# A folded Fourier mixer: modulation sums spread anew, pairs of tiles folded in two operations, the two pairs leaving in the other order

## The chip, the cores and the metric

The kernel runs on one core of one Trainium2 chip. The metric is the device time of one execution in microseconds (us). Three runs of the kernel before gave 2249.22, 2250.83 and 2252.3 us; the median is 2250.83 us. The profile is of one execution of its own.

## The reference

One inference step of a two-layer backbone over 128 context tokens and 512 latent tokens of 1024 channels, in float32. Every layer is a half-step SwiGLU feed-forward part (hidden width 2816), a token mixer, and another half-step feed-forward part. Each of these six sub-layers is wrapped in the same frame:

```
h = rmsnorm(x, g_pre) * (1 + scale) + shift
x = x + gate * rmsnorm(sublayer(h), g_post)
```

Shift, scale and gate come from `silu(cond) @ w_mod + b_mod`, nine vectors of 1024 per layer, one set for the context tokens and one for the latent tokens. The mixer of layer 0 is a Fourier mixer: `u = h @ w_in`, then the real part of a two-dimensional discrete Fourier transform over the positions of a sequence and the 128 channels of each of eight groups, then `@ w_out`; context and latent tokens are separate sequences. The mixer of layer 1 is attention. The outputs are the tokens and the keys and values of the context tokens.

## The kernel before

The six sub-layers are numbered n = 0 to 5; n = 1 is the Fourier mixer and n = 4 the attention. The 640 tokens are five tiles of 128: tiles 0, 1, 3 and 4 hold latent tokens, tile 2 the context. Every float32 product is three matmuls on pieces: `split` (L258) rounds a value on ScalarE (hi, L260) and takes the rest on VectorE (lo, L261), and `mm3` (L271) multiplies hi by hi, hi by lo and lo by hi (L274 to L276).

**Weights.** All weights of the program stand in one list of units of 512 KB. `unit(i)` (L204) hands out unit i and first sends those up to three further on: `send` (L211) starts a load into one of four raw buffers (`raw_tile`, L199, on the SP queue, in order), combines columns where the unit asks for it (L226 to L228, L236, L238, L243) and splits the result into one of six weight buffers, or, where its kind has "block" in it, into two tiles of a general ring of twenty. The ring holds hidden values and tokens as well.

**Modulation sums.** One vector of 128 outputs of `w_mod` is one "sum" here: a load of 512 KB into a raw buffer, and for each of the two conditions one VectorE operation over 1024 elements (`gemv`, L471 to L476). 128 of them wait in a list (`background`, L1589 to L1595), and `behind(n)` (L253) issues the next n. Before, this happens only in the feed-forward parts: after each tile of the first four slices of the second product, `BEHIND[n]` in all per part (L44, L956).

**A feed-forward part** (`ffn`, L728) goes through 22 hidden chunks; after every fourth chunk its part of the second product runs for all five tiles (`w2`, L905), and after the last six chunks for tiles (0, 1), (2), (3) and (4). The end of a tile hands its two PSUM banks to `boundary`, which starts a chain.

**A chain** (`chain`, L608) is the frame above for one tile: squares and their sum (L620), gate (L621, L624), root on GpSimd (L597), the new x (L627), squares of it (L641), the multiplication by the inverse root (L644), eight transposes on TensorE (L665), then scale and shift (L686 on ScalarE, L688 on VectorE), and the split into the next sub-layer's h. The result stands in `wide_y`, 1024 columns per tile. `TURNS` (L45) says after how many ns of matmul work the transposes are put into TensorE's order. From n = 0 to n = 1 the tokens of tiles 0 and 1, and of 3 and 4, are also folded into their difference and sum (L650, L651) before the transposes, and the second tile of a pair gets the scale without the shift (L680, L682). Tile 0 keeps its x in four pieces, so each operation on it is four.

**The Fourier mixer** (`fourier`, L1068): `pair_in(0)` multiplies pair (0, 1) by the folded `four_in` (L236 and L238 fold its columns; two operations of L238, one for each half of the groups), then the context, then `pair_in(1)`. `positions(m)` and `channels(m)` do the transform for four m, each a position step ahead of the channel step. Then the product with eight units of `four_out`: `own` (the even rows of the context, L1234), `pair_out(0)`, the odd rows of the context (`ctx`, L1240), `pair_out(1)`; each is followed by the chains of its tiles. The next feed-forward part takes tiles 0, 1 and half of tile 2 first (`finish(0)`, L942, then 320 columns), the others later.

The order on each engine is not the order of the text alone: a scheduler places what is ready by priority, `high_priority` (all of a chain) ahead of the rest, and `behind_of` or `issue_after` ties an instruction behind another. Each engine then goes through its order and waits at each instruction for what it needs.

## Time and profile before

| what | us |
|---|---|
| median of three runs | 2250.83 |
| the profiled execution's own time | 2249.42 |
| span of the profiled execution | 2247.6 |
| TensorE (PE) busy | 2173.4 |
| VectorE (DVE) busy | 1753.9 |
| ScalarE (ACT) busy | 1175.2 |

The rows below come from views of this one execution. A row of the windows view names a stretch (us from the start of the span) and its length, then the busy time and number of instructions of PE, PE's weight loads, DVE, ACT and GpSimd (POOL), the granted clock of TensorE as a share of full speed, the share of the DMA engines, and GB/s. A row of the groups view names line, engine, operation, the tiles written and read, the shape and count, then busy us, mean ns of one, and idle us before them. A row of the timeline has start and duration in us and, in brackets, the idle time before it and what ended it. A row of the waits view names who waited for whom, us in all, times and the longest.

### The profile page before, as it was taken

How to read it: one execution, taken by the hardware profiler on the slowest of the kernel's cores; microseconds unless marked ns; L12 is line 12 of the kernel's file. 1: busy time of each engine (PE TensorE's matmuls, PEld its weight loads, DVE VectorE, ACT ScalarE, POOL GpSimd, SP SyncE). 2: the span in 40 equal slices, each digit the busy share in tenths (PEclk: the TensorE clock that was granted, in tenths of full speed). 3: DMA queues.
4: the chain of work that ended last, by engine and by line, in shares of the span. 5: the costliest groups of instructions: out<-in, count | busy, mean ns of one | idle time of the engine just before them, and what ended most of it. 6: DMA issues, size and time to landing. Idle time of an engine off the chain costs nothing.

```text
span 2247.6 us, 34637 instructions
## 1 busy us (share of the span) xinstructions
PE 2173.4 (97%) x13299; PEld 1999.0 (89%) x13299; DVE 1753.9 (78%) x3255; ACT 1175.2 (52%) x2222; POOL 44.4 (2%) x95
## 2 busy tenths in 40 slices
PE   7999899898989999999999999999999999999998
PEld 5989889886689999998999999989999899999997
DVE  5988988978788898896988998776555686766684
ACT  4534444454654554545545545466788654455452
POOL 0000000000000000000000000000000000000000
PEclk9999999998989999999999999999999999999999
DMA  8244344434324344444334344523333323322232
GB/s 311 86 158 169 123 151 159 150 107 133 115 81 155 127 158 143 136 160 150 117 132 147 130 149 156 192 82 96 116 110 113 102 92 103 113 91 88 94 127 99
DMA packets 85862, 293.25 MB, mean 130 GB/s; under 512 B 9696, under 2 KB 14656, under 8 KB 85568
## 3 DMA queue, kind: packets, MB, share of 16 engines
q1 hardware_dynamic: 85152, 290.39, 38.6%
q8 instruction: 104, 1.70, 0.3%
q10 hardware_dynamic: 544, 0.66, 0.1%
q14 instruction: 62, 0.51, 0.1%
HBM read 275.49 MB, written 11.58 MB: 128 GB/s over the span
## 4 chain that ended last, share of the span: by engine, by line
PE 82%; DVE 9%; DMA 4%; ACT 3%; issue 2%; POOL 0%; SPq 0%; DVEq 0%; POOLq 0%; ACTq 0%
PE main L274 11%; PE main L275 11%; PE main L276 11%; PE score L274 7%; PE score L276 7%; PE score L275 7%; PE turn L274 4%; PE turn L275 4%; PE turn L276 4%; PE sum L276 4%; PE sum L275 4%; PE sum L274 4%; DVE junk L473 3%; DMA raw<-in_w_mod_t 2%; DVE lo L261 2%
## 5 line engine op out<-in xcount | busy, mean ns | idle before, releaser
L260 ACT ACTIVATE hi<-raw 128x1024 fp32r<-128x1024 f32 (+1 forms) x388 | 370.8, 968 | 291.5 <-PE score L275 88.6
L261 DVE TENSOR_TENSOR lo<-raw,hi 128x1024 fp32r<-128x1024 f32 (+1 forms) x388 | 429.2, 1113 | 105.2 <-ACT hi L260 103.6
L275 PE MATMUL main<-lo,ring 128*128 128x512 f32 (+5 forms) x1089 | 408.8, 376 | 8.1 <-DVE lo L261 8.1
L274 PE MATMUL main<-hi,ring 128*128 128x512 f32 (+4 forms) x1089 | 411.1, 379 | 2.0 <-DVE ring L627 1.2
L276 PE MATMUL main<-hi,ring 128*128 128x512 f32 (+5 forms) x1089 | 407.8, 375 | 0.0
L473 DVE SCALAR_TENSOR_TENSOR junk<-raw,wide 128x1024 bf16<-128x1024 f32 x256 | 313.1, 1223 | 77.5 <-DMA raw<-in_w_mod_t 73.5
L274 PE MATMUL score<-ring,hi 128*128 128x320 f32 x916 | 287.3, 314 | 16.6 <-ACT hi L260 12.2
L276 PE MATMUL score<-ring,lo 128*128 128x320 f32 x916 | 287.0, 313 | 6.0 <-DVE lo L261 5.8
L275 PE MATMUL score<-ring,hi 128*128 128x320 f32 x916 | 286.0, 312 | 0.0
L275 PEld LDWEIGHTS main<-lo,ring 128*128 128x128 f32 (+2 forms) x1089 | 204.7, 188 | 47.2 <-DVE lo L261 9.2
L274 PEld LDWEIGHTS main<-hi,ring 128*128 128x128 f32 (+2 forms) x1089 | 203.7, 188 | 43.6 <-DVE ring L627 1.4
L276 PEld LDWEIGHTS main<-hi,ring 128*128 128x128 f32 (+2 forms) x1089 | 204.6, 188 | 40.0 <-issue 0.6
L274 PE MATMUL turn<-ring,hi 128*128 128x320 f32 x672 | 208.6, 310 | 0.1
L275 PE MATMUL turn<-ring,hi 128*128 128x320 f32 x672 | 208.4, 310 | 0.0
L274 PE MATMUL sum<-ring,hi 128*128 128x320 f32 x672 | 207.5, 309 | 0.3 <-DVE left L868 0.3
L275 PE MATMUL sum<-ring,hi 128*128 128x320 f32 x672 | 207.7, 309 | 0.0
L276 PE MATMUL sum<-ring,lo 128*128 128x320 f32 x672 | 207.7, 309 | 0.0
L276 PE MATMUL turn<-ring,lo 128*128 128x320 f32 x672 | 207.5, 309 | 0.0
L929 ACT ACTIVATE y<-main 128x512 f32<-128x512 f32 x160 | 94.2, 591 | 208.9 <-PE main L276 207.7
L274 PEld LDWEIGHTS score<-ring,hi 128*128 128x128 f32 x916 | 175.0, 191 | 19.9 <-ACT hi L260 13.4
L276 PEld LDWEIGHTS score<-ring,lo 128*128 128x128 f32 x916 | 174.6, 191 | 8.1 <-DVE lo L261 8.1
L275 PEld LDWEIGHTS score<-ring,hi 128*128 128x128 f32 x916 | 175.2, 191 | 0.7
(312 smaller groups left out, 4123.6 us busy)
## 6 DMA issues: line engine op xcount, KB each, us to landing
raw<-in_w SPq DMA_DIRECT2D x272, 512.0 KB, 3.8
raw<-in_w_mod_t SPq DMA_DIRECT2D x128, 512.0 KB, 3.5
raw<-in_qkv SPq DMA_DIRECT2D x26, 512.0 KB, 3.5
spill<-ring SPq DMA_DIRECT2D x12, 640.0 KB, 3.0
ring<-spill SPq DMA_DIRECT2D x12, 640.0 KB, 7.3
raw<-in_bias SPq DMA_DIRECT2D x16, 448.0 KB, 3.8
first<-in_w_mod_k SPq DMA_DIRECT2D x8, 512.0 KB, 8.3
ring<-in_w_mod_k SPq DMA_DIRECT2D x8, 512.0 KB, 10.2
```

What stands on the lines that cost most here:

```text
L260: a = self.nc.scalar.activation(hi, src, AF.Copy)
L261: self.last_split = a, self.nc.vector.tensor_tensor(lo, src, hi.bitcast(F32), op=ALU.subtract)
L274: mm(out, whi, xhi, start=start, stop=False)
L275: mm(out, whi, xlo, start=False, stop=False)
L276: self.latest = mm(out, wlo, xhi, start=False, stop=stop)
L473: last = self.nc.vector.scalar_tensor_tensor(out=self.junk, in0=raw, scalar=1.0, in1=self.wide[:, cond, :], op0=ALU.mult, op1=ALU.mult, ac ...
L929: nc.scalar.activation(place(i, a), ps[a], AF.Copy)
```

## The change

- `BEHIND` of the first feed-forward part goes from 48 to 36. The twelve sums are issued elsewhere: four in the last slice of the same part's second product, three in `pair_in(1)`, five in the loop over `channels`.
- The fold of a pair of tiles takes two operations that multiply by the inverse root at the same time, one for the difference and one for the sum, in place of a multiplication and two operations. The difference has the other sign; the sine matrix `diffs` is negated for it. The first tile of a pair, tile 2, and in the Fourier mixer's chains tile 3, are multiplied by the inverse root on ScalarE.
- After the transposes of a pair the first tile's eight scale-and-shift operations are all on ScalarE; the second tile's eight become two on VectorE, one for each PSUM bank, with the scale read with a stride of zero. The splits of a pair cover both tiles in one.
- The inner columns of `four_in` are stored with the two halves of the groups interleaved, so that the second fold operation is one; the even columns are cut at 256 and 520 rather than at 260 and 520. The cosine and sine matrices of the channel step are stored to match.
- `pair_out(1)` comes first, then `own`, `ctx` and `pair_out(0)`. Tiles 3 and 4 take the columns 0 to 255 of the next h and tiles 0 and 1 the last 256 (`SWAPPED`, `slot`); the next feed-forward part begins with tiles 3, 4 and 2.
- Of `four_out`, units 3 and 4 lie in the ring in place of 6 and 7, and the loop over `channels` calls for units 0 to 3 (and with them up to unit 6).
- `TURNS` has a row of its own for n = 0 and n = 1; the transposes of pair (3, 4) in n = 0 and of tiles 2, 3 and 4 in n = 1 come later.

The core of the diff:

```diff
 SLICES = ((0, 4), (4, 8), (8, 12), (12, 16), (16, 22))
 EARLY = 2
-BEHIND = (48, 0, 36, 36, 0, 8)
+BEHIND = (36, 0, 36, 36, 0, 8)
 TURNS = (
+    {1: 15500, 2: 9200, 4: 15500},
+    {0: 10500, 1: 14000, 2: 10500, 3: 12500, 4: 15500},
     {0: 10500, 1: 14000, 2: 9200, 3: 11000, 4: 13000},
-    {1: 15500, 2: 9200, 4: 12500},
...
 CTX_TILE = 2
+SWAPPED = (3, 4, 2, 0, 1)
...
             raw = self.raw_tile(src)
             a, b = raw[:, one], raw[:, two]
             if "rows" not in kind:
-                a = raw[:, :528].rearrange("p (a x) -> p a x", a=2)[:, :, :256].rearrange("p a (g c) -> p a g c", c=64)
-                a, b = a[:, :, :, 1:], raw[:, 520:].rearrange("p (a g c) -> p a g c", a=2, c=63)
+                a, b = a.rearrange("p (m c) -> p m c", m=4)[:, :, 2:], raw[:, 520:].rearrange("p (m c) -> p m c", m=4)
             nc.vector.tensor_tensor(b, a, b, op=ALU.subtract)
-            for x, y in [(a, b)] if "rows" in kind else [(a[:, i], b[:, i]) for i in range(2)]:
-                nc.vector.scalar_tensor_tensor(out=x, in0=x, scalar=2.0, in1=y, op0=ALU.mult, op1=ALU.subtract)
+            nc.vector.scalar_tensor_tensor(out=a, in0=a, scalar=2.0, in1=b, op0=ALU.mult, op1=ALU.subtract)
...
-    def finish(self, half):
-        for i in ((0, 1, 2), (3, 4))[half]:
-            self.close(i)
+    def finish(self, half, first=(0, 1, 2)):
+        for i in range(TILES):
+            if (i in first) == (not half):
+                self.close(i)
...
+    def slot(self, n, i):
+
+        return SWAPPED[i] if n == 2 else i
...
-        place = self.wide_y[:, i * D : (i + 1) * D]
+        slot = self.slot(n + 1, i)
+        place = self.wide_y[:, slot * D : (slot + 1) * D]
...
-            for t, lo, hi in x:
-                nc.vector.tensor_scalar_mul(place[:, lo:hi], t, r)
             pair = next((p for p in PAIRS if i in p), None) if n == 0 else None
-            if pair and i == pair[0]:
-                return
-            if pair:
-                a, b = (self.wide_y[:, j * D : (j + 1) * D] for j in pair)
-                tt(b, a, b, op=ALU.subtract)
-                nc.vector.scalar_tensor_tensor(out=a, in0=a, scalar=2.0, in1=b, op0=ALU.mult, op1=ALU.subtract)
-                if i == pair[1] == 1:
+            if pair and i == pair[1]:
+                first, t = self.wide_y[:, pair[0] * D : i * D], x[0][0]
+                nc.vector.scalar_tensor_tensor(out=place, in0=t, scalar=r, in1=first, op0=ALU.mult, op1=ALU.subtract)
+                nc.vector.scalar_tensor_tensor(out=first, in0=t, scalar=r, in1=first, op0=ALU.mult, op1=ALU.add)
+                if i == 1:
                     k = self.coef[:, 0, 1, 0, 0]
                     tt(self.twice, k, k, op=ALU.add)
-        yield TURNS[n == 0][i]
-        tiles = pair or (i,)
+            else:
+                for t, lo, hi in x:
+                    if n == 0 or n == 1 and i == 3:
+                        copy(place[:, lo:hi], t, AF.Copy, scale=r)
+                    else:
+                        nc.vector.tensor_scalar_mul(place[:, lo:hi], t, r)
+                if pair:
+                    return
+        yield TURNS[min(n, 2)][i]
+        tiles = pair or (slot,)
...
+                if pair and j == pair[1]:
+                    for a, bank in enumerate(banks):
+                        to = y[:, :, 4 * a : 4 * a + 4].rearrange("p v c t -> p c v t")
+                        k = self.coef[:, 0, 1, 1, 0, 4 * a : 4 * a + 4].unsqueeze(2).unsqueeze(3)
+                        t = bank.rearrange("p (c v t) -> p c v t", c=4, t=64)
+                        tt(to, t, k.to_broadcast([P, 4, 2, 64]), op=ALU.mult)
+                    continue
                 for c in range(NCH):
                     k = self.coef[:, layer, sub, :, int(i == CTX_TILE), c : c + 1]
                     to, t = y[:, :, c], pieces(banks[c // 4][:, c % 4 * P : (c % 4 + 1) * P])
                     if n == 3:
                         to, t = rows_of(j)[:, c, :: -1 if j in (0, 4) else 1], banks[c // 4][:, c % 4 * P : (c % 4 + 1) * P]
-                    if pair and j == pair[1]:
-                        if c < 4:
-                            copy(to, t, AF.Copy, scale=k[:, 1])
-                        else:
-                            nc.vector.tensor_scalar_mul(to, t, k[:, 1])
-                        continue
                     bias = self.twice[:, c : c + 1] if pair else k[:, 0]
-                    if c < 4:
+                    if c < 4 or pair:
                         copy(to, t, AF.Identity, bias=bias, scale=k[:, 1])
                     else:
                         nc.vector.tensor_scalar(to, t, k[:, 1], bias, op0=ALU.mult, op1=ALU.add)
...
-                for j in tiles:
-                    y = self.staged[:, 2 * j : 2 * j + 2][:, :: -1 if j == CTX_TILE else 1]
-                    for c in range(0, NCH, 2):
-                        hi, lo = (h.block(part, c, 0)[:, :, FIRST_COLS[j] : FIRST_COLS[j] + P] for part in range(2))
-                        split = lambda b: b.rearrange("p c (v t) -> p c v t", t=64)
-                        self.ready = self.split(split(hi), split(lo), y[:, :, c : c + 2].rearrange("p v c t -> p c v t"))
+                j, n_pieces = tiles[0], 2 * len(tiles)
+                y = self.staged[:, 2 * j : 2 * j + n_pieces][:, :: -1 if j == CTX_TILE else 1]
+                for c in range(0, NCH, 2):
+                    hi, lo = (h.block(part, c, 0)[:, :, FIRST_COLS[j] : FIRST_COLS[j] + 64 * n_pieces] for part in range(2))
+                    split = lambda b: b.rearrange("p c (v t) -> p c v t", t=64)
+                    self.ready = self.split(split(hi), split(lo), y[:, :, c : c + 2].rearrange("p v c t -> p c v t"))
...
                 w = self.unit(base + w2_at[s] + f - f0)
+                if n == 0 and s == len(SLICES) - 1 and tiles[0] == 0 and f < f0 + 4:
+                    self.behind()
                 for i in tiles:
-                    at = i * P if n else FIRST_COLS[i]
+                    at = self.slot(n, i) * P if n else FIRST_COLS[i]
...
-                    self.finish(half)
+                    self.finish(half, (3, 4, 2) if n == 2 else (0, 1, 2))
...
-                    self.units += [("foldrowsblock" if u >= NWU else "foldrows", io["four_out"][u]) for u in range(NCH)]
+                    self.units += [("foldrowsblock" if u in (3, 4) else "foldrows", io["four_out"][u]) for u in range(NCH)]
...
-        main_at = (0, 128, 264, 392, 256)
+        main_at = (0, 128, 256, 384, 512)
+        parts_of = ((0, 256), (256, 520))
...
             for k in range(NCH):
+                if p and k % 3 == 1:
+                    self.behind()
                 even_in(k, token(k, 256 * p, 256 * p + P), es)
                 odd_in(k, token(k, 256 * p + P, 256 * p + 256), o)
...
         for m in range(4):
             following = positions(m + 1) if m < 3 else None
+            self.behind((2, 2, 1, 0)[m])
+            self.unit(at + 3 + m)
             channels(m, *ready)
             ready = following
...
-            ts = [self.wide_y[:, j * D + a * WIDE : j * D + (a + 1) * WIDE] for a in halves]
+            ts = room(self.slot(2, j))
...
+        pair_out(1)
         own = [self.bank("score") for _ in halves]
         for a in halves:
-            even_out(a, 0, 66, own[a])
-            with high():
-                copy(rest[a][64:66], own[a][64:66], AF.Copy)
-        pair_out(0)
-        ctx = [self.bank(kind) for kind in ("turn", "sum")]
-        for a in halves:
-            odd_out(a, 0, ctx[a])
+            with self.behind_of(self.latest):
+                even_out(a, 0, 66, own[a])
             with high():
                 copy(rest[a][:64], own[a][:64], AF.Copy)
                 copy(rest[a][64:], own[a][:64], AF.Copy)
                 copy(rest[a][64:65], own[a][64:65], AF.Copy)
+                copy(special[a][64:66], own[a][64:66], AF.Copy)
+        ctx = [self.bank(kind) for kind in ("turn", "sum")]
+        for a in halves:
+            with self.behind_of(self.latest):
+                odd_out(a, 0, ctx[a])
+            with high():
                 tt(ctx[a], ctx[a], rest[a], op=ALU.add)
         boundary(2, ctx)
-        pair_out(1)
+        pair_out(0)
...
-    out["four_in"] = cont(np.concatenate([flat(win[:, :, :4, :64]), flat(win[:, :, :, 64]), flat(win[:, :, 4:, :64]),
-                                          flat(win[..., mirror[1:]])], axis=2))
+    inner = win.reshape(NCH, P, 4, 2, GROUP).transpose(0, 1, 2, 4, 3)
+    out["four_in"] = cont(np.concatenate([flat(inner[:, :, :, :64]), flat(win[:, :, :, 64]),
+                                          flat(inner[:, :, :, mirror[1:]])], axis=2))
...
```

More of the change, by code (lines that the diff above doesn't have):

```diff
@@ L1097, in pair_in @@
             with high():
-                for a in range(2):
-                    self.split(hi[:, a * 260 : a * 260 + 260], lo[:, a * 260 : a * 260 + 260], es[a][:, :260])
+                for e, (a, b) in zip(es, parts_of):
+                    self.split(hi[:, a:b], lo[:, a:b], e[:, : b - a])
                 self.split(hi[:, 520:1024], lo[:, 520:1024], o[:, :504])
@@ L1115, in fourier @@
             copy(plain, odd[:64, :504], AF.Copy)
-            for a in range(2):
-                self.split(ends[0][:, a * 260 : a * 260 + 260], ends[1][:, a * 260 : a * 260 + 260], even[a][:66, :260])
+            for e, (a, b) in zip(even, parts_of):
+                self.split(ends[0][:, a:b], ends[1][:, a:b], e[:66, : b - a])
         self.close(4)
@@ L1217, in pair_out @@
                 if not p:
-                    self.latest = mm(far[a][:4], small[64:66, 204:208], rest[a][64:66], start=False, stop=True,
+                    self.latest = mm(far[a][:4], small[64:66, 204:208], special[a][64:66], start=False, stop=True,
                                      skip_group_check=True)
```

19 lines of the change are left out of this document (10 added, 9 removed).

## The prediction

> **What bounds the kernel now.** First the page, for the span and the engines:
>
> ```profile
> span 2247.6 us, 34637 instructions
> PE 2173.4 (97%) x13299; PEld 1999.0 (89%) x13299; DVE 1753.9 (78%) x3255; ACT 1175.2 (52%) x2222; POOL 44.4 (2%) x95
> raw<-in_w_mod_t SPq DMA_DIRECT2D x128, 512.0 KB, 3.5
> ```
>
> PE is busy for 97% of the span. The change removes no matmul, so all that it can win lies in the time in which PE waits, and in the time in which its clock is granted at half. Where those lie, the view of busy time by stretches says. The stretches are the first feed-forward part from its start-up on, its last slice, the Fourier mixer with its chains, and the two feed-forward parts n = 2 and 3:
>
> ```profile
> 57.00:460.00 403.00, 380.61 (x2228) 354.24 (x2227) 354.72 (x587) 182.54 (x288) 0.00 (x0) 0.97 0.43 143
> 460.00:490.00 30.00, 30.00 (x132) 24.34 (x131) 21.07 (x46) 10.49 (x29) 2.68 (x5) 1.00 0.37 141
> 490.00:650.00 160.00, 137.06 (x742) 112.44 (x742) 126.84 (x244) 91.65 (x202) 9.73 (x15) 0.91 0.32 106
> 650.00:1480.00 830.00, 830.00 (x4939) 774.27 (x4939) 715.99 (x1188) 411.92 (x682) 8.70 (x17) 1.00 0.42 141
> ```
>
> Length less PE's busy time: 22.4 us of idle in n = 0, 22.9 in the Fourier stretch, nothing at all in the 830 us of n = 2 and 3. The clock falls in the same two places: (1 - 0.97) x 403 = 12 us lost at most in n = 0 and (1 - 0.91) x 160 = 14 in the mixer. A part of this falls on idle time and costs nothing.
>
> Who ends the idle time, I read in the view of waits, PE alone, of the first and of the third stretch, then in the timeline of DVE at the end of the first slice:
>
> ```profile
> PE score L274 <- ACT hi L260: 12.2, 4, 4.0
> PE score L276 <- DVE lo L261: 5.2, 3, 4.4
> ...
> 149.63 1.22 DVE L473 SCALAR_TENSOR_TENSOR junk<-raw,wide 128x1024 bf16<-128x1024 f32 x1
> ...
> 153.35 0.69 DVE L243 SCALAR_TENSOR_TENSOR raw<-sums,raw 128x512 f32<-128x512 f32 x1
> 154.44 1.23 DVE L261 TENSOR_TENSOR lo<-sums,hi 128x1024 fp32r<-128x1024 f32 x1 [0.40 <-ACT hi L260]
> ```
>
> In n = 0 PE waits for split weights. The weights are late because DVE makes their column sums (L226 to L243) only after the last modulation sum (L473, here until 150.8). The count of these operations in a slice of n = 0 and in one of n = 2:
>
> ```profile
> 100.00:155.00 55.00, 29.53 (x48) 1.00 0.42 144
> 660.00:740.00 80.00, 22.15 (x36) 1.00 0.39 132
> ```
>
> Two conditions and two records each: 12 sums a slice against 9, so 2.46 us of DVE per sum. With 12 PE loses 22.4 / 4 = 5.6 us per slice; with 9 nothing.
>
> **The change, part by part.**
>
> *Twelve sums leave n = 0.* Each slice gets three sums fewer, 7.4 us less on DVE and three loads fewer on SP, against 5.6 us to win: the idle 22.4 us should go. The half clock after it goes too. Of its 12 us I take 10, since some falls in idle stretches. Gain 32.4. The rows of n = 2 are the ground: same slices, same nine sums. Below, if half of the 7.4 us only reaches PE: 4 x 3.7 = 14.8, and half of the clock, 20.
>
> *Four of them go into the last slice of n = 0.* They cost 4 x 2.46 = 9.8 us of DVE, which has 30.0 - 21.07 = 8.9 idle there, under 30 us of uninterrupted matmuls. Their four loads go ahead of those of `four_in` on SP. Without the cover they would delay tile 0's chain. I take 1 us lost, between 0 and 9.8.
>
> *Entry into the mixer.* Here the same views show:
>
> ```profile
> 500.00:509.60 9.60, 7.88 (x40) 6.39 (x39) 9.05 (x22) 7.12 (x20) 1.54 (x2) 1.00 0.35 109
> 509.60:513.00 3.40, 3.40 (x9) 2.12 (x9) 2.96 (x9) 3.33 (x12) 0.59 (x1) 0.51 0.14 17
> 520.00:534.00 14.00, 9.60 (x40) 7.15 (x41) 13.96 (x29) 5.77 (x10) 0.00 (x0) 0.64 0.36 115
> ...
> 519.53 3.66 DVE L261 TENSOR_TENSOR ring<-y,ring 128x256 fp32r<-128x256 f32 x13
> 523.10 1.22 DVE L261 TENSOR_TENSOR lo<-raw,hi 128x1024 fp32r<-128x1024 f32 x1
> ...
> 524.38 0.58 PE L275 MATMUL main<-lo,ring 128*128 128x260 f32 x1 [6.66 <-DVE lo L261]
> ```
>
> DVE is the bound (9.05 of 9.6, 13.96 of 14). PE waits 9.6 - 7.88 = 1.7 us and then 6.66 for a weight that stands on DVE behind thirteen splits of the chain. The clock costs 0.49 x 3.4 = 1.7 and, of 0.36 x 14 = 5.0, some 2.9 while PE works. In all 13.0. What DVE is spared, from the groups of 475 to 534 us:
>
> ```profile
> L644 DVE TENSOR_SCALAR y<-ring,col 128x1024 f32<-128x1024 f32 x4 | 3.0, 754 | 2.2 <-POOL col L605 2.2
> L644 DVE TENSOR_SCALAR y<-ring,col 128x256 f32<-128x256 f32 x4 | 1.1, 350 | 0.0
> L651 DVE SCALAR_TENSOR_TENSOR y<-y 128x1024 f32<-128x1024 f32 x2 | 2.4, 1222 | 0.0
> L682 DVE TENSOR_SCALAR y<-score,coef 128x128 f32<-128x128 f32 x8 | 2.4, 345 | 0.2 <-PE score L665 0.2
> L688 DVE TENSOR_SCALAR y<-sum,coef,sk 128x128 f32<-128x128 f32 x8 | 2.7, 404 | 0.0
> L621 DVE TENSOR_TENSOR main<-main,total 128x512 f32<-128x512 f32 x3 | 2.1, 694 | 0.2 <-ACT y L620 0.2
> L641 ACT ACTIVATE y<-ring 128x1024 f32<-128x1024 f32 x4 | 4.2, 1054 | 2.5 <-DVE ring L627 2.5
> ```
>
> All multiplications by the root leave DVE: 3.0 + 1.1 = 4.1 us. The fold stays at two operations of two sources (L651, 1.22 each, L650 the same kind). Sixteen small operations (2.4 + 2.7) become four that read a bank, by L621 about 0.69 each: 5.1 - 2.8 = 2.3. In all 6.4 us. Merged splits and the single fold operation handle as many elements as before; I count them at nothing, DVE's total being what matters. The operations with a stride of zero are not in the trace; I take L621, and 0.35 to 1.22 bounds the four within 2 us. ACT gets three multiplications, 3 x 1.05 by L641, where it was busy 7.12 of 9.6 us, so it eats part of this. The later transposes of pair (3, 4) put 3 us more of matmuls ahead of the wait. I leave 2 us of idle and one half clock of 1.7 standing: gain 13.0 - 3.7 = 9.3, between 0 (ACT or the later turn takes it back) and 13.
>
> *Eight sums go into `pair_in(1)` and `channels`, and `four_out` changes its buffers.* What room there is, and what comes after:
>
> ```profile
> 534.00:558.00 24.00, 23.21 (x161) 20.79 (x161) 14.80 (x21) 11.59 (x18) 0.00 (x0) 1.00 0.44 146
> 558.00:574.00 16.00, 16.00 (x96) 12.89 (x95) 13.39 (x24) 7.00 (x16) 0.00 (x0) 1.00 0.28 89
> 574.00:587.00 13.00, 13.00 (x56) 8.67 (x56) 8.75 (x11) 7.93 (x12) 0.00 (x0) 1.00 0.81 266
> 587.00:614.00 27.00, 26.42 (x118) 20.14 (x117) 20.12 (x42) 19.75 (x46) 2.93 (x6) 1.00 0.19 69
> 614.00:634.00 20.00, 6.83 (x32) 6.16 (x31) 18.85 (x36) 10.68 (x25) 3.59 (x5) 0.66 0.41 145
> ```
>
> Eight sums are 8 x 2.46 = 19.7 us. DVE has 9.2 + 2.6 + 4.3 = 16.1 idle from 534 to 587, where all of `four_out` has to be folded and split: 3.6 short. The three in `pair_in(1)` (7.4) fit into 9.2. The five of `channels` (12.3) do not fit into 2.6; they stand in the program's order ahead of units 3 to 6 of `four_out`, and their loads use the same four raw buffers and the same SP queue as those units. Units 3 and 4 in the ring no longer wait for the cosine and sine weights to leave their buffers, which works against the loss. I take 4 us of new waiting for late `four_out` units near the second half of the first pair, plus 1.7 of clock: loss 5.7. Bounds: 0, if the scheduler lets the sums drift past 587 where DVE is idle for another 6.9, and 12.3 - 2.6 = 9.7 plus 1.7 = 11.4.
>
> *The order of leaving.* PE stops at 614 for 20 - 6.83 = 13.2 us. The timeline around its end:
>
> ```profile
> 613.40 0.15 DVE L602 TENSOR_SCALAR col<-col 128x1 f32<-128x1 f32 x1 [0.40 <-ACT y L641]
> ...
> 621.91 1.41 DVE L627 SCALAR_TENSOR_TENSOR ring<-main,col,ring 128x512 f32<-128x512 f32 x2 [0.55 <-POOL col L605]
> ...
> 624.43 0.75 DVE L644 TENSOR_SCALAR y<-ring,col 128x1024 f32<-128x1024 f32 x1
> ...
> 626.05 1.09 PE L665 MATMUL turn<-ident,y 128*128 128x128 f32 x4 [11.76 <-DVE y L644]
> ```
>
> Tile 2's root is begun at 613.4, but its multiplication runs at 624.4, behind the chains of tiles 3 and 4, and 11.76 us of PE end with it. Now `own` (2 x 13 matmuls, at 13.0 / 56 = 0.23 us each 6.0 us) stands behind the first pair, so that pair's chains begin 6 us earlier, and run while `own` and `ctx` cover them; DVE was idle for 6.9 of the 27 us there. Tile 0 with its pieces is in the last pair, which the next part needs only after the first half's matmuls; 144 of them lie between (830 / 4939 = 0.168 us each, 24 us), and cover its turns at 10.5 and 14 us. That is why I count the swapped columns at nothing. Tile 2 still ends only some 15 us before PE needs it, and now competes with chains of tiles 0 and 1. Of 13.2 + 0.6 (587 to 614) idle and of the 0.34 x 20 = 6.8 of clock, of which I take 2.5 while PE works, 16.3 in all, I leave 4 us of idle and 1.7 of clock: gain 10.6, between 0 and 16.3.
>
> *The sum*, against the profiled execution's own 2249.42 us: - 32.4 + 1 - 9.3 + 5.7 - 10.6 = - 45.6, so 2203.8. The median of the runs is 1.4 above the profiled one: 2205.2, and I say 2206.
>
> [...] The row of 509.6 to 513 has the clock at 0.51 after 1.7 us of idle, hence my 1.7 for each. [...]
>
> **The rivals.**
>
> *All waiting goes.* The scheduler finds room for every sum and the last chain is early: - 32.4 - 13.0 - 16.3 + 1 leaves 2188.7, with the 1.4 about 2190. For it: n = 2 and 3 show that DVE at 716 of 830 us needn't stop PE. Against: DVE at 13.39 of 16 in `channels` before five sums are added.
>
> *Short waits cost no clock.* As forecast without three times 1.7: 2206 - 5 = 2201. The trace has one row against it.
>
> *DVE becomes the bound of the mixer.* The five sums cost their upper bound, 11.4, and with DVE late neither the entry nor the end wins: 2249.4 - 31.4 + 11.4 + 1.4 = 2231. For it: 12.3 us into 2.6. Against: those three places are each released by different work.
>
> *The first part doesn't gain.* If the late weights of n = 0 come from the four raw buffers and not from the sums, its 32.4 stay, and the change doesn't do what it says: 2249.4 + 1 - 9.3 + 5.7 - 10.6 + 1.4 = 2238. Against: 830 us without a wait at nine sums a slice.
>
> *Slower.* Place: the SP queue between 534 and 587. A load of a sum waits for a raw buffer and holds up every load behind it, `four_out` among them; if each of the eight then costs its landing and its DVE time in full, 3.5 + 2.46, that is 47.7, and the end stays as late as it was: 2249.4 - 31.4 - 9.3 + 47.7 + 1.4 = 2258. It decides from 40.7 / 8 = 5.1 us exposed per sum. Against: PE works without a stop from 558 to 587 and the loads of `four_out` have been running ahead of it.
>
> **How the numbers follow.** Chances: the forecast 0.44, all waiting gone 0.18, no clock price 0.10, the mixer bound by DVE 0.18, no gain in the first part 0.05, slower 0.05. Two rivals on each side of the forecast hold most of the rest, so the range goes from 2188 (all gone) to 2232 (mixer bound by DVE) and leaves out about 0.1. A difference under 0.2%, 4.5 us, can't be told from none here. Faster holds all cases but the last, less 0.02 for what may pile up to nothing: 0.93; same 0.02; slower 0.05.
>
> **What would show it.** Right in the first part: no wait of PE for ACT hi or DVE lo between 57 and 460, clock 1.00, nine sums a slice. Right at the entry: the 6.66 us wait at about 518 is under 2, and no L644 on DVE there. Right in the middle: a wait on a `four_out` split between the channel step and the second half of `pair_out(1)`; none means the sums fit. Right at the end: the wait for L644 before the next part falls from 11.76 to about 4. It is wrong if n = 0 keeps waits of 4 us, if tile 2's chain is again queued for 10 us on DVE, or if the last pair, needed later, becomes the next wait of n = 2.

## The result: 31.5 us faster, with a new loss in the middle of the mixer

The changed kernel takes 2218.47 us (median of four runs, 2217.1 to 2220.75), beside 2250.02 for the kernel before (2248.84 to 2252.3): a ratio of 0.986, with a 95% interval of 0.9842 to 0.9877. The forecast was 2206, so of some 44 us it was to win, 31.5 came.

The page of the changed kernel:

```profile
span 2216.7 us, 34573 instructions
PE 2173.2 (98%) x13299; PEld 1997.3 (90%) x13299; DVE 1743.1 (79%) x3218; ACT 1179.2 (53%) x2221; POOL 45.3 (2%) x95
```

PE has the same matmuls and the same busy time as before (2173.2 against 2173.4), so the 30.9 us of span are idle time of PE: it falls from 2247.6 - 2173.4 = 74.2 us to 43.5. A matmul at half clock is busy for longer (in the trace after, one of 512 columns takes 0.63 us in the stretch with the clock at 0.50 and 0.39 us soon after it), so what the clock costs stands within the busy time, and in sum it hasn't shrunk: what it gave up in n = 0 it took in the middle, as the rows below say. To compare the two I cut both traces at about the same four places: the first feed-forward part (n = 0) without its last slice, the entry into the mixer, the middle (`pair_in(1)`, the position and channel steps, the start of the product with `four_out`), and the leaving (from the end of the first pair into the next part). The view of busy time by stretches, first of the kernel before:

```profile
57.00:480.00 423.00, 400.61 (x2315) 370.51 (x2314) 368.02 (x613) 187.97 (x303) 0.55 (x1) 0.97 0.43 146
480.00:540.00 60.00, 51.59 (x258) 41.15 (x257) 52.38 (x117) 34.66 (x90) 5.35 (x9) 0.89 0.22 71
540.00:587.00 47.00, 46.21 (x269) 37.06 (x267) 34.02 (x49) 24.68 (x40) 0.00 (x0) 1.00 0.48 157
587.00:640.00 53.00, 39.26 (x189) 32.30 (x188) 41.99 (x81) 30.43 (x70) 6.52 (x10) 0.87 0.28 100
```

and of the kernel after, where the third number after the length is DVE's busy time and the third from the end the granted clock:

```profile
57.00:445.00 388.00, 387.86 (x2317) 362.20 (x2316) 344.38 (x565) 188.21 (x300) 0.55 (x1) 1.00 0.44 148
445.00:505.00 60.00, 54.49 (x291) 44.17 (x290) 51.98 (x98) 39.33 (x92) 6.23 (x9) 0.94 0.25 81
505.00:566.00 61.00, 54.49 (x243) 42.32 (x242) 53.05 (x89) 24.08 (x42) 0.00 (x0) 0.80 0.54 181
566.00:610.00 44.00, 40.26 (x194) 31.74 (x193) 34.82 (x70) 30.41 (x67) 6.56 (x10) 0.92 0.32 109
```

Length less PE's busy time is idle; (1 - clock) times the length is at most what the clock took:

| stretch | before: idle + clock | after: idle + clock at most | forecast gain | gain |
|---|---|---|---|---|
| n = 0 | 22.4 + 10 (as the prediction took it) | 0.1 + 0 | 32.4 | 32.3 |
| entry | 8.4 + 4.6 (as predicted) | 5.5 + 3.6 | 9.3 | 3.9 |
| middle | 0.8 + 0 | 6.5 + 12.2 | -5.7 | -17.9 |
| leaving | 13.8 + 2.5 (as predicted) | 3.7 + 3.5 | 10.6 | 9.1 |

The four gains make 27.4 of the 30.9 us. The column of before takes the part of the clock that the prediction counted, the column of after all that it can be; with all of it in both, n = 0 gains 34.9, the entry 5.9 and the leaving 13.4, and the four make 36.3. The 30.9 lie between. The view of waits of PE after (445 to 610) names what it now waits for; in n = 0 the same view is empty:

```profile
PE main L275 <- DVE lo L261: 3.9, 2, 3.4
PE turn L274 <- ACT ring L260: 2.9, 1, 2.9
PE main L274 <- ACT hi L260: 2.3, 1, 2.3
PE score L274 <- DVE ring L261: 1.9, 1, 1.9
PE main L274 <- DVE rms L261: 1.8, 1, 1.8
```

The wait of 11.76 us for the multiplication of tile 2 is gone; the 2.9 at the next part's first matmul is what is left of it. The 6.66 at the entry is 3.4. New are three short waits of 1.8 to 2.3 us in the middle, around the position and channel steps and at the first pair's second half, and with them the clock at 0.80. The timeline after has them one by one. Its two rows of DVE show what runs ahead of the second: L478 is the operation of a sum in this kernel, and the matmul of 539.49 waits for the split of 538.95:

```profile
522.10 0.39 PE L274 MATMUL main<-hi,ring 128*126 128x256 f32 x1 [1.77 <-DVE rms L261]
...
537.81 1.22 DVE L478 SCALAR_TENSOR_TENSOR junk<-raw,wide 128x1024 bf16<-128x1024 f32 x1
...
538.95 0.49 DVE L261 TENSOR_TENSOR ring<-score,ring 128x322 fp32r<-128x322 f32 x1
...
539.49 0.41 PE L274 MATMUL score<-left,hi 128*128 128x322 f32 x1 [1.85 <-DVE ring L261]
...
560.00 0.73 PE L274 MATMUL main<-hi,ring 128*128 128x512 f32 x2 [2.35 <-ACT hi L260]
```

The first two are a position step and a channel step that wait for a short split on DVE, in the second case one that stands right behind a sum. Only the third is a wait for a weight of `four_out`. DVE itself waits for the load of a sum for only 0.2 us in these 61 us, and for no load of `four_out`, by its own view of waits (505 to 566), of which this is the only row with a load:

```profile
DVE junk L478 <- DMA raw<-in_w_mod_t: 0.2, 1, 0.2
```

So the lateness that this trace shows is the sums' time on DVE and not their loads; no run separates the two.

### The profile page after: what moved, and what is told of

It reads as the page before. It is cut to its first block, busy times and chain, and to the rows that moved or that the text cites. A ratio compares the mean times of both kernels' runs of the same rounds, so it can differ in the third digit from the quotient of the medians.

```text
span 2216.7 us, 34573 instructions
## 1 busy us (share of the span) xinstructions
PE 2173.2 (98%) x13299; PEld 1997.3 (90%) x13299; DVE 1743.1 (79%) x3218; ACT 1179.2 (53%) x2221; POOL 45.3 (2%) x95
## 4 chain that ended last, share of the span: by engine, by line
PE 89%; DVE 5%; ACT 3%; DMA 2%; issue 1%; POOL 0%; SPq 0%; DVEq 0%; POOLq 0%; ACTq 0%
PE main L275 12%; PE main L276 12%; PE main L274 12%; PE score L275 7%; PE score L276 7%; PE score L274 7%; PE turn L275 4%; PE turn L274 4%; PE sum L274 4%; PE sum L275 4%; PE turn L276 4%; PE sum L276 4%; DVE junk L478 1%; DMA raw<-in_w_mod_t 1%; PE sum L1569 1%
## 5 line engine op out<-in xcount | busy, mean ns | idle before, releaser
L261 DVE TENSOR_TENSOR lo<-raw,hi 128x1024 fp32r<-128x1024 f32 (+1 forms) x388 | 429.7, 1112 | 99.1 <-ACT hi L260 97.7
L275 PE MATMUL main<-lo,ring 128*128 128x512 f32 (+4 forms) x1089 | 410.8, 378 | 4.8 <-DVE lo L261 4.8
L478 DVE SCALAR_TENSOR_TENSOR junk<-raw,wide 128x1024 bf16<-128x1024 f32 x256 | 313.1, 1223 | 79.6 <-DMA raw<-in_w_mod_t 75.5
L275 PE MATMUL score<-ring,hi 128*128 128x320 f32 x916 | 283.7, 310 | 0.0
L274 PE MATMUL score<-ring,hi 128*128 128x320 f32 x916 | 283.3, 309 | 0.0
L274 PEld LDWEIGHTS score<-ring,hi 128*128 128x128 f32 x916 | 172.4, 188 | 1.1
L275 PEld LDWEIGHTS score<-ring,hi 128*128 128x128 f32 x916 | 172.3, 188 | 0.7
```

Of the source, the lines that this page charges most:

```text
L261: self.last_split = a, self.nc.vector.tensor_tensor(lo, src, hi.bitcast(F32), op=ALU.subtract)
L274: mm(out, whi, xhi, start=start, stop=False)
L275: mm(out, whi, xlo, start=False, stop=False)
L478: last = self.nc.vector.scalar_tensor_tensor(out=self.junk, in0=raw, scalar=1.0, in1=self.wide[:, cond, :], op0=ALU.mult, op1=ALU.mult, ac ...
```

## The experiments

The theory after the result: the twelve sums made n = 0 wait, and five of them, put into the channel loop, cost the mixer some 17 us. The rivals: the moved buffers of `four_out` made the new waits; or the order of leaving did nothing. All the kernels below were timed beside the kernel before, whose median was 2247.8 to 2250.0 us in each comparison, so the ratios are what to compare. The last two columns are of the profiled execution: PE's busy time, which grows with half clock (0.63 us in place of 0.39 for the matmul above), and its idle time, the span less the busy time.

| kernel | median us | ratio to before, 95% interval | PE busy | PE idle |
|---|---|---|---|---|
| as changed | 2218.47 | 0.9860 (0.9842 to 0.9877) | 2173.2 | 43.5 |
| all sums back | 2236.03 | 0.9944 (0.9927 to 0.9961) | 2172.8 | 61.2 |
| only the sums moved | 2233.28 | 0.9928 (0.9913 to 0.9943) | 2169.8 | 62.3 |
| order back | 2219.05 | 0.9867 (0.9852 to 0.9882) | 2163.3 | 51.1 |
| fold back | 2224.73 | 0.9891 (0.9876 to 0.9905) | 2172.8 | 51.5 |
| `four_out` buffers back | 2216.97 | 0.9861 (0.9846 to 0.9876) | 2168.6 | 47.5 |
| one sum in the channel loop | 2218.10 | 0.9865 (0.9841 to 0.9889) | 2167.6 | 50.0 |
| five sums in hidden chunks | 2213.50 | 0.9844 (0.9825 to 0.9863) | 2168.7 | 45.8 |
| eight sums in hidden chunks | 2207.15 | 0.9818 (0.9802 to 0.9833) | 2162.4 | 41.4 |
| the same, order back | 2214.26 | 0.9847 (0.9829 to 0.9865) | 2161.7 | 50.8 |
| the same, fold back | 2212.12 | 0.9834 (0.9819 to 0.9849) | 2161.8 | 48.4 |
| the same, delays back | 2207.51 | 0.9816 (0.9799 to 0.9834) | 2162.8 | 43.2 |
| the same, `four_in` splits first | 2206.72 | 0.9813 (0.9796 to 0.9829) | 2161.1 | 43.8 |

**All sums back.** The changed kernel, with the twelve sums where they were:

```diff
-BEHIND = (36, 0, 36, 36, 0, 8)
+BEHIND = (48, 0, 36, 36, 0, 8)
...
-                if n == 0 and s == len(SLICES) - 1 and tiles[0] == 0 and f < f0 + 4:
-                    self.behind()
...
-                if p and k % 3 == 1:
-                    self.behind()
...
-            self.behind((2, 2, 1, 0)[m])
```

> The changed kernel with all 48 sums back in the slices of the first feed-forward part; everything else as changed. Theory (the twelve sums make the waits of n = 0 when they are there, and five of them make the waits of the channel step when they are there): n = 0 waits again for about 22 us and loses 10 of clock, the stretch from pair_in(1) to the first pair loses its new waits (6.5 us idle, about 12 of clock): 2218 + 32 - 17 = 2233 us, no sum in the mixer and no wait of PE for a four_out split. Rival (the new waits in the mixer come from the units 3 and 4 of four_out in the ring and their early calls): the waits around the channel step stay, 2218 + 32 = 2250 us.

It took 2236.03 us. Its stretches n = 0 and middle:

```profile
57.00:480.00 423.00, 400.61 (x2325) 370.99 (x2324) 368.86 (x614) 189.90 (x310) 0.55 (x1) 0.98 0.44 146
540.00:583.00 43.00, 41.96 (x234) 34.09 (x233) 36.41 (x53) 22.94 (x40) 0.00 (x0) 1.00 0.51 172
```

The 22.4 us of idle in n = 0 are back to the hundredth, and the middle, with the buffers of `four_out` as changed, has 1.0 us of idle and a full clock. So the sums make both, and the moved buffers alone do not make the loss.

**Only the sums moved.** The kernel before with the three calls above added:

```diff
-BEHIND = (48, 0, 36, 36, 0, 8)
+BEHIND = (36, 0, 36, 36, 0, 8)
```

> The kernel before with nothing changed but where the twelve sums are issued (36 in the slices, 4 in the last slice, 3 in pair_in(1), 5 in the channel loop). Theory: n = 0 gains 32 us, the channel step and four_out lose about 17 by late splits and half clock, the entry and the end wait as before: 2250 - 32 + 17 = 2235 us. Rival (the sums cost the mixer nothing, the other edits do): 2250 - 32 = 2218 us.

It took 2233.28 us, 15.7 less than before. Its stretches n = 0, entry, middle and leaving:

```profile
57.00:448.00 391.00, 390.22 (x2326) 363.80 (x2325) 346.17 (x572) 189.83 (x309) 0.55 (x1) 1.00 0.44 147
448.00:507.00 59.00, 47.34 (x231) 36.78 (x231) 53.03 (x121) 33.76 (x84) 4.96 (x9) 0.91 0.22 71
507.00:580.00 73.00, 64.92 (x338) 49.20 (x336) 60.64 (x101) 31.92 (x60) 0.54 (x1) 0.97 0.49 160
580.00:625.00 45.00, 32.16 (x149) 27.97 (x150) 34.36 (x68) 23.18 (x51) 5.09 (x9) 0.74 0.33 117
```

The whole 32 us of n = 0 are won by the sums alone, and half of it is paid back. The total is as expected, its place is not: here the middle has 8.1 us of idle and at most 2.2 of clock; the entry, with DVE busy for 53.03 of 59 us, has 11.7 us of idle where it had 8.4; and the leaving has 12.8 of idle where it had 13.8, but at most 11.7 of clock where it had 6.9. The sums are worth 15.7 us alone and 2236.03 - 2218.47 = 17.6 on top of the other edits, so the two groups of edits nearly add up.

**Order back.** The changed kernel with the order of leaving, the columns, the delays of the Fourier chains and tile 3's multiplication as before (the main lines; the calls of the last stage are those of the kernel before):

```diff
-SWAPPED = (3, 4, 2, 0, 1)
+SWAPPED = (0, 1, 2, 3, 4)
...
-    {0: 10500, 1: 14000, 2: 10500, 3: 12500, 4: 15500},
+    {0: 10500, 1: 14000, 2: 9200, 3: 11000, 4: 13000},
...
-                    if n == 0 or n == 1 and i == 3:
+                    if n == 0:
...
-        pair_out(1)
         own = [self.bank("score") for _ in halves]
...
+        pair_out(0)
...
         boundary(2, ctx)
-        pair_out(0)
+        pair_out(1)
```

> The changed kernel with the order of leaving as before (own, pair_out(0), ctx, pair_out(1)), the columns not swapped, the delays of the Fourier chains as before and tile 3 multiplied on DVE. Theory: the wait at the start of the next feed-forward part comes back to some 10 to 12 us with its half clock, 2218 + 10 = 2228 us. Rival (that wait fell because DVE has less to do, not by the order): 2218 to 2220 us.

It took 2219.05 us, no different from the changed kernel, so by time the rival holds. The trace says otherwise. Its middle and its leaving, and its longest wait:

```profile
505.00:570.00 65.00, 60.36 (x288) 44.72 (x288) 56.95 (x98) 31.14 (x63) 0.72 (x2) 0.95 0.52 170
570.00:610.00 40.00, 26.88 (x142) 23.38 (x141) 32.78 (x63) 21.63 (x44) 4.91 (x9) 0.79 0.37 131
...
PE turn L675 <- DVE y L662: 9.4, 1, 9.4
```

The wait for tile 2 is back at 9.4 us, and the leaving has 13.1 us of idle in place of 3.7. But the middle has only 4.6 of idle and at most 3.3 of clock, in place of 6.5 and 12.2. What the new order wins at the end, it gives back in the middle: against the changed kernel, PE's idle time is 7.6 us longer and its busy time 9.9 shorter. The second wait of the middle is 0.67 us here, though a sum stands right ahead of the split on DVE (536.60) as it does there. No wait of 535 to 550 is longer, and the clock stays full:

```profile
538.28 0.42 PE L274 MATMUL score<-left,hi 128*128 128x322 f32 x1 [0.67 <-DVE ring L261]
...
535.00:550.00 15.00, 13.32 (x56) 9.01 (x55) 14.96 (x30) 5.71 (x10) 0.00 (x0) 1.00 0.60 191
```

Two runs further down show on what that hangs.

**Fold back.** The changed kernel with the chains from n = 0 to the mixer as before (the main lines; the splits again one for each tile):

```diff
-                nc.vector.scalar_tensor_tensor(out=place, in0=t, scalar=r, in1=first, op0=ALU.mult, op1=ALU.subtract)
-                nc.vector.scalar_tensor_tensor(out=first, in0=t, scalar=r, in1=first, op0=ALU.mult, op1=ALU.add)
+                nc.vector.tensor_scalar_mul(place, t, r)
+                tt(place, place, first, op=ALU.subtract)
+                nc.vector.scalar_tensor_tensor(out=first, in0=first, scalar=2.0, in1=place, op0=ALU.mult, op1=ALU.add)
...
-                    if n == 0 or n == 1 and i == 3:
+                    if n == 1 and i == 3:
...
-                        tt(to, t, k.to_broadcast([P, 4, 2, 64]), op=ALU.mult)
...
+                        if c < 4:
+                            copy(to, t, AF.Copy, scale=k[:, 1])
+                        else:
+                            nc.vector.tensor_scalar_mul(to, t, k[:, 1])
```

> The changed kernel with the chains from n = 0 to the mixer as before: multiplications by the root on DVE, three operations for a pair's fold, sixteen scale operations of a pair shared between ACT and DVE, a split per tile. Theory: 6.4 us more of DVE work ahead of the four_in split of the entry, of which the wait there grows from 3.4 to 7 us or more: 2218 + 4 to 7 = 2222 to 2225 us. Rival (the entry is set by the order of the splits and by ACT, not by the sum of DVE work): within 2 us of 2218.

It took 2224.73 us, 6.3 more than as changed. Its entry:

```profile
446.00:506.00 60.00, 52.42 (x260) 41.18 (x259) 54.09 (x117) 34.84 (x92) 5.22 (x9) 0.91 0.23 74
```

DVE is busy for 54.09 of 60 us instead of 51.98, and 7.6 us are idle instead of 5.5, with at most 5.4 of clock instead of 3.6. The time is just within the theory's range and outside the rival's. Over the whole span DVE is busy for 1748.7 us instead of 1743.1, so the edit costs DVE 5.6 us, near the 6.4 worked out. But the wait that was to grow to 7 us didn't: the longest of the entry is 2.2 us, and the one at the first position step grows from 1.8 to 4.3. The time came as worked out; the wait by which it was to come did not.

**`four_out` buffers back.** Units 6 and 7 in the ring again, and no early calls:

```diff
-                    self.units += [("foldrowsblock" if u in (3, 4) else "foldrows", io["four_out"][u]) for u in range(NCH)]
+                    self.units += [("foldrowsblock" if u >= NWU else "foldrows", io["four_out"][u]) for u in range(NCH)]
...
-            self.unit(at + 3 + m)
```

> The changed kernel with units 6 and 7 of four_out in the ring as before and no early calls for them in the channel loop. Theory (early units 3 and 4 soften the lateness that the sums make): the wait for a four_out split at the second half of pair_out(1) grows from 2.9 to 5 us or more, 2218 + 3 to 8 = 2221 to 2226 us. Rival (the early folds and splits are themselves what delays the channel step): its waits go, 2208 to 2215 us.

2216.97 us: neither theory's number. This edit can't be told from none. In the middle the idle grows from 6.5 to 8.9 and the clock's part falls from at most 12.2 to at most 5.9; over the whole span PE idles for 4.0 us more and is busy for 4.6 less:

```profile
508.00:562.00 54.00, 45.07 (x220) 34.80 (x219) 50.31 (x83) 21.86 (x37) 0.00 (x0) 0.89 0.57 194
```

**One sum in the channel loop**, ten in each slice of n = 0:

```diff
-BEHIND = (36, 0, 36, 36, 0, 8)
+BEHIND = (40, 0, 36, 36, 0, 8)
...
-            self.behind((2, 2, 1, 0)[m])
+            self.behind((1, 0, 0, 0)[m])
```

> The changed kernel with 40 sums in the slices of n = 0 (ten each), four in the last slice, three in pair_in(1) and one in the channel loop. Theory (ten sums a slice are 2.46 us more than nine, which have no wait, and less than the 5.6 us wait of twelve; four sums fewer in the channel step win most of its loss): n = 0 loses 0 to 6 us, the mixer wins 10 to 15: 2205 to 2214 us. Rival (the wait of a slice begins at once above nine sums): n = 0 loses 10 or more with its half clock, 2215 to 2220 us.

2218.1 us (2214.36 to 2222.84), no gain. The time is the rival's, the loss in n = 0 is the theory's. Its n = 0 and its middle:

```profile
57.00:450.00 393.00, 387.75 (x2303) 361.05 (x2302) 349.60 (x577) 184.42 (x296) 0.00 (x0) 1.00 0.44 150
515.00:565.00 50.00, 44.70 (x234) 36.28 (x234) 42.72 (x69) 22.61 (x38) 0.00 (x0) 0.94 0.53 178
```

With ten sums a slice n = 0 idles for 5.3 us, between 0.1 with nine and 22.4 with twelve: nine is where the slice is full. The middle with four sums still has 5.3 of idle and at most 3.0 of clock, so the three sums of `pair_in(1)`, which the prediction let pass free of charge, seem to have a price too; one sum of the channel loop is still there, so this run alone doesn't show it.

**Eight sums in hidden chunks.** The mixer holds no sum at all; the eight are issued in n = 0, each behind a hidden chunk and not in a slice:

```diff
                 w1_fast(a, half)
+                if n == 0 and a in (6, 7, 10, 11, 14, 15, 18, 19):
+                    self.behind()
...
-                if p and k % 3 == 1:
-                    self.behind()
...
-            self.behind((2, 2, 1, 0)[m])
```

> The changed kernel with the eight sums of the mixer issued in n = 0 instead, one behind each of the hidden chunks 6, 7, 10, 11, 14, 15, 18 and 19. Theory (the sums in the channel step cost some 17 us there, most of it half clock): the mixer is as in the run with all sums back, without a wait between the channel step and the first pair, and n = 0 has 45 us of DVE idle for 19.7 us of sums: 2218 - 17 = 2201 us, up to 2208 if the chunks with a sum wait now and then. Rival (n = 0 has no room for them, each costs its 2.46 us there): 2218 - 17 + 20 = 2221 us.

2207.15 us, 11.3 less than as changed and the best of the kernels up to here. Its four stretches:

```profile
57.00:450.00 393.00, 391.01 (x2326) 363.94 (x2325) 359.72 (x598) 189.10 (x309) 0.55 (x1) 1.00 0.46 156
450.00:507.00 57.00, 50.43 (x269) 40.52 (x268) 50.64 (x97) 36.91 (x84) 6.24 (x9) 0.94 0.25 84
507.00:555.00 48.00, 46.89 (x262) 37.99 (x261) 38.88 (x59) 26.30 (x46) 0.54 (x1) 1.00 0.45 154
555.00:597.00 42.00, 38.21 (x187) 30.40 (x186) 33.42 (x68) 29.33 (x65) 6.03 (x9) 0.92 0.34 113
```

The middle is down to 1.1 us of idle at full clock, and n = 0 pays 2.0 us for eight sums more, with DVE busy for 359.72 of 393 us.

**Five sums in hidden chunks**, the three of `pair_in(1)` kept:

```diff
+                if n == 0 and a in (7, 11, 15, 18, 20):
+                    self.behind()
...
-            self.behind((2, 2, 1, 0)[m])
```

> The changed kernel with only the five sums of the channel loop issued in n = 0, behind the chunks 7, 11, 15, 18 and 20; the three of pair_in(1) stay. Theory (the three fit into DVE's idle time, the five do not): the same gain as without any sum in the mixer, 2201 to 2205 us. Rival (the three cost as much each as the five): 3/8 of the 17 us stay, 2207 to 2212 us.

2213.5 us (2210.14 to 2216.27), outside the theory's range and 1.5 above the rival's. Its n = 0 and middle:

```profile
57.00:450.00 393.00, 389.20 (x2310) 362.45 (x2309) 350.77 (x580) 183.76 (x297) 0.00 (x0) 1.00 0.45 152
515.00:565.00 50.00, 47.69 (x243) 37.64 (x242) 42.06 (x69) 24.88 (x45) 0.54 (x1) 0.93 0.50 169
```

The middle loses 2.3 of idle and at most 3.5 of clock, where that of the kernel with eight sums in hidden chunks loses 1.1 and nothing: that is the price of the three, at most 4.7 us, and with the 1.8 that n = 0 loses more it comes near the 6.4 us between the two kernels. The wait of 1.8 us at the first position step, which the kernel with eight sums in hidden chunks doesn't have, is back. And n = 0 idles for 3.8 us with five sums where it idled for 2.0 with eight, so in n = 0 the number of sums alone doesn't set the price, their place counts as well; which place is the bad one isn't settled.

**Eight in hidden chunks, order back.** The edits of the two kernels together:

> The kernel with the eight sums in the hidden chunks (2207 us) and the order of leaving as in the kernel before. Theory (the new order wins some 10 us at the end, and where the sums stand in the channel step it gives them back there because the first pair asks for all of four_out at once): without sums in the mixer nothing is given back, and the old order costs 8 to 12 us: 2215 to 2219 us, with a wait of about 10 us for the multiplication of tile 2. Rival (the order is worth nothing in either case): 2205 to 2209 us.

2214.26 us against 2207.15: without sums in the mixer the new order is worth 7.1 us, a little less than the theory's 8 to 12. Its middle and leaving, and its longest wait:

```profile
507.00:560.00 53.00, 52.41 (x276) 39.90 (x275) 37.84 (x55) 29.38 (x51) 0.54 (x1) 1.00 0.42 140
560.00:605.00 45.00, 31.21 (x160) 27.41 (x159) 36.95 (x73) 24.87 (x56) 6.04 (x9) 0.81 0.32 117
...
PE turn L675 <- DVE y L662: 11.9, 1, 11.9
```

The leaving idles for 13.8 us, as in the kernel before, and the middle is clean with either order (0.6 and 1.1 us). So the order's gain at the end is real, and the changed kernel gives it back only while the sums stand in the mixer.

**Eight in hidden chunks, fold back:**

> The kernel with the eight sums in the hidden chunks (2207 us) and the chains from n = 0 to the mixer as in the kernel before. Theory (the new chain spares DVE 6.4 us at the entry and about 4 of it reach PE): the waits of the entry grow by 3 to 6 us, 2210 to 2213 us. Rival (without sums in the mixer the entry's lateness is made up before the channel step): within 2 us of 2207.

2212.12 us, 5.0 more, as the theory had it. Over the whole span DVE is busy for 7.0 us more (1748.1 against 1741.1). The entry idles for 12.15 us in place of 6.6, with one wait of 8.17 before a `four_in` matmul whose weight isn't yet rounded:

```profile
445.00:510.00 65.00, 52.85 (x263) 41.44 (x262) 60.40 (x129) 35.88 (x93) 6.40 (x10) 0.92 0.26 83
...
492.42 0.80 PE L274 MATMUL main<-hi,ring 128*128 128x256 f32 x2 [8.17 <-ACT hi L260]
```

**Eight in hidden chunks, delays back** (both rows of `TURNS` with the numbers of before):

```diff
-    {1: 15500, 2: 9200, 4: 15500},
-    {0: 10500, 1: 14000, 2: 10500, 3: 12500, 4: 15500},
+    {1: 15500, 2: 9200, 4: 12500},
+    {0: 10500, 1: 14000, 2: 9200, 3: 11000, 4: 13000},
```

> The kernel with the eight sums in the hidden chunks (2207 us) and the delays of the transposes as in the kernel before (12500 for pair (3, 4) from n = 0; 9200, 11000 and 13000 for tiles 2, 3 and 4 of the mixer), the new order kept. Theory (the wait at the entry is a split queued on DVE behind the pair's splits, the one at the end is tile 2's own chain; the delays only say where in PE's order the transposes stand): within 3 us of 2207, the wait at the entry of 3.7 us longer by up to 3. Rival (the later transposes are what won at the entry and at the end): 2212 us or more.

2207.51 us: the later transposes are worth nothing that can be measured.

**Eight in hidden chunks, `four_in` splits first:**

```diff
-        self.split(hi, lo, raw[:, at])
+        with self.tc.high_priority() if kind in ("fold", "foldblock") else ExitStack():
+            self.split(hi, lo, raw[:, at])
```

> The kernel with the eight sums in the hidden chunks (2207 us) and the splits of four_in at the priority of a chain. Theory (the entry's wait of 3.7 us is one split of four_in queued on DVE behind the splits of the pair, and not a lack of DVE time): that wait falls under 1 us and takes its half clock of 3 us along, 2201 to 2204 us. Rival (DVE is full there, so the wait moves to the transposes of the pair or to the next split): 2206 us or more.

2206.72 us, no gain: the rival. The order on DVE changed, and one wait of 6.4 us took the place of those of 3.7 and 1.1 (the lines of this kernel are one higher, L261 is the rounding on ACT):

```profile
483.04 0.58 PE L275 MATMUL main<-hi,ring 128*128 128x256 f32 x1 [6.40 <-ACT ring L261]
```

PE now waits for the splits of the tokens in place of one of a weight. That fits an entry that lacks DVE time, as does the price of the fold; that no other order would do better isn't shown by one.

## Why the prediction was partly right

The time is 12.5 us above the forecast and within the range, which was wide (2188 to 2232) because rivals on both sides held a chance. Two of the four large terms came near to what was forecast, two did not, and both of these erred to the same side.

*Twelve sums leave n = 0* (gain 32.4): right in mechanism and size. 0.1 us of idle and a clock of 1.00 are left; the sums alone win it, and putting them back brings 22.4 us of idle back. The 10 us of clock are borne out too: the kernel with all sums back and the one with eight in hidden chunks both have a full clock in the middle, and PE is busy for 2172.8 us in the one and 2162.4 in the other. Nine sums a slice is the edge, as the rows of n = 2 and 3 had it.

*Four go into the last slice* (loss 1): no run separates it. The entry of the kernel with all sums back has 60.00 - 53.72 = 6.3 us of idle, by the row

```profile
480.00:540.00 60.00, 53.72 (x293) 43.77 (x292) 45.68 (x84) 38.61 (x85) 5.34 (x9) 0.97 0.22 71
```

against 5.5 as changed, but at most 1.8 of clock against 3.6. Taken together that is 1.0 worse as changed, which is the size forecast, but one execution of each can't settle so little.

*Entry* (gain 9.3): the mechanism was right, the size was not: 3.9 by the rows, 5.0 to 6.3 by the two kernels with the fold back. The 6.4 us that DVE was to be spared hold: the fold back costs it 5.6 and 7.0, and the four operations with a stride of zero, which the prediction took at 0.69 us, take 0.686:

```profile
L688 DVE TENSOR_TENSOR y<-score,coef 128x512 f32<-128x512 f32 x4 | 2.6, 686 | 0.7 <-PE score L675 0.7
```

They came through to PE at most one for one, and the step that failed is the leap from there to 2 us of idle left: the wait of 6.66 was to fall under 2 and is 3.37, and ahead of it DVE is still busy without a gap:

```profile
478.00:483.00 5.00, 1.68 (x9) 0.84 (x7) 5.00 (x11) 0.13 (x2) 0.00 (x0) 0.94 0.24 93
```

The 3 us of cover that the later transposes of pair (3, 4) were to give, and the order of the splits, change nothing that the time shows.

*Eight sums in the mixer* (loss 5.7, bound 11.4): this is the term that was mis-sized. It measured at most 17.9 by the rows. By the times, taking the eight sums out of the mixer won 11.3 us in all, after 2.0 us paid for them in n = 0, so they cost the mixer some 13. Three things in the step failed. The waiting was put at late weights of `four_out` near the second half of the first pair; 2.35 and 0.53 us of it are there, but 1.77 and 1.85 stand at short splits of the position and channel steps, which the prediction didn't price. The three sums of `pair_in(1)` were said to fit into 9.2 us of DVE idle; they cost time (five sums in hidden chunks). And I priced the clock at 1.7, one stretch of 3.4 us at half, where it took up to 12.2; by PE's busy time with and without the eight sums (2173.2 and 2162.4), 10.8. The view of two neighbouring stretches after; the wait of 1.85 us, which ends at 539.49, is in the first:

```profile
537.00:540.40 3.40, 1.55 (x8) 0.91 (x6) 3.40 (x7) 1.06 (x1) 0.00 (x0) 1.00 0.45 154
540.40:554.00 13.60, 13.60 (x35) 9.56 (x35) 12.00 (x26) 4.18 (x7) 0.00 (x0) 0.50 0.58 181
```

Soon after the 1.85 us without work the clock stands at half for 13.6 us, in which PE is busy throughout. That is not all loss: DVE is busy for 12.0 of those 13.6 us, so with a full clock PE would have waited for DVE in part. I read idle and half clock as two faces of one late engine here, which would also be how the kernel with the `four_out` buffers back has more idle, less of half clock and the same time; no run shows it.

*Order of leaving* (gain 10.6): right at its place, 9.1 by the rows, and 11.76 us of waiting for tile 2 became 2.9. But taken alone it moved the time by nothing, since the middle gives it back while the sums are there; the prediction treated the two as separate terms. Without the sums it is 7.1 us. Why the old order meets the sums with less half clock is shown only this far: its waits there are shorter (0.67 us at most, where one is 1.85).

*Nothing for swapped columns*: right; PE has no wait from 600 to 1480, so n = 2 opens without one for tiles 0 and 1. The moved buffers, which were to work against the loss, and the delays are worth nothing by the runs without them.

*The clock after the waits left standing* (1.7 for each of three, by the row of 509.6 to 513): no run shows one price for each. By the rows after, the clock took at most 3.6 us at the entry, 12.2 in the middle and 3.5 at the leaving. What the runs say of it stands at the end.

Of the rivals, "DVE becomes the bound of the mixer" came closest to the truth: the middle went past its price of 11.4, while the entry and the end won all the same. The rival of the SP queue finds no support: DVE waited 0.2 us for a load in the middle.

## What to carry to other kernels

Background work moved off a full stretch costs where it lands, and the place where the engine is least busy on average isn't the place for it: the same eight sums cost some 13 us in the mixer, where DVE was busy for 72% of the middle before (34.02 of 47 us), and 2.0 us spread singly over hidden chunks of a part in which DVE was already at 89%. That the engine has idle time for the work in sum isn't enough where PE waits for each of its short results: `pair_in(1)` had 9.2 us of DVE idle for the 7.4 of three sums, and they still had a price, at most 4.7 us. When two edits are close in time, price them together; here the gain of one was paid out only once the other was gone.

## What the runs showed of the hardware

Half clock followed some waits of under 2 us in these traces. In the kernel with five sums in hidden chunks one wait of 1.79 us (528.70 to 530.50), with PE fully busy in the 2.7 us ahead of it, was followed by 6.8 us at half clock:

```profile
526.00:528.70 2.70, 2.70 (x18) 2.16 (x17) 2.67 (x4) 1.79 (x4) 0.00 (x0) 1.00 0.44 152
528.70:531.40 2.70, 0.91 (x8) 0.77 (x7) 2.67 (x6) 1.32 (x2) 0.00 (x0) 1.00 0.96 290
531.40:538.20 6.80, 6.80 (x25) 5.75 (x24) 4.20 (x7) 1.00 (x3) 0.00 (x0) 0.50 0.40 136
```

Here and after the wait of 1.85 us in the changed kernel, the clock fell about 0.9 us after work had begun again (at 531.40 and 540.40). The half clock lasted 6.8 us here, 13.6 in the changed kernel and 3.4 at 509.6 in the kernel before. So the waits of 1.79 and 1.85 us can have cost more in clock (at most 3.4 and 6.8 us) than in idle. (The 1.7 us of idle ahead of 509.6, which the prediction read as one wait, are two, of 0.57 and 1.15 us.) Not every such wait had one behind it: after one of 1.24 us in the changed kernel, which ends at 473.91, the clock is 1.00 up to 480.70, and it is 1.00 too after one of 1.84 us in the kernel with eight sums in hidden chunks and the fold back:

```profile
456.81 0.50 PE L274 MATMUL main<-hi,ring 128*128 128x512 f32 x1 [1.84 <-ACT main L913]
...
456.81:460.20 3.39, 3.39 (x14) 2.64 (x15) 3.39 (x10) 1.67 (x3) 0.48 (x1) 1.00 0.02 5
460.20:463.60 3.40, 3.40 (x16) 2.73 (x16) 2.92 (x7) 1.96 (x3) 0.56 (x2) 1.00 0.45 154
```

What decides between them isn't shown.
